# Where the last feed-forward keeps its split weights, where the context gates are applied, and which queue copies the latent keys

## The chip, the cores and the metric

The kernel runs on one core of one Trainium2 chip. The metric is the device time of one execution in microseconds (us); the time before is the median of three runs. One execution was also profiled, and all rows below are from that one. The engines are PE (TensorE: MATMUL, and PEld for its weight loads), DVE (VectorE), ACT (ScalarE), POOL (GpSimd) and SP (SyncE, which issues most of the DMA transfers).

## The reference, cut to what matters

A first block runs on 512 tokens of width 1024: a mixer, a cross attention and a mixture of 16 experts. A second block of two layers follows, on two streams at once: the latent tokens (512, the first block's output) and the context tokens (256). Each layer modulates, projects, attends in three ways (a gated linear attention, a neighborhood attention with 6 heads, "na", and a grouped-query attention with 2 key heads, "ga"), and then does

```python
o = token_mixers(modulate(x, sh1, sc1), ...)   # 1024 wide; the same for the context rows xc
x = layer_norm(ALPHA * x + g1 * (o @ w_out), ln1_g, ln1_b)
a, b = split(modulate(x, sh2, sc2) @ w_ffn_in) # 2 x 2816 wide
x = layer_norm(ALPHA * x + g2 * ((silu(a) * b) @ w_ffn_out), ln2_g, ln2_b)
```

g1 and g2 are rows of 1024 gate factors. The context stream does all of this in layer 0 only; in layer 1 only its keys and values are needed. The latent stream does it in both layers, and the last thing that the program computes is the latent feed-forward of layer 1, here called the last feed-forward.

## The kernel before, in words

**Products.** Every operand is kept as two fp32r parts, high and low, whose sum is the fp32 value, and a product takes three matmuls (`mm3`, L343): high·high, high·low, low·high. A weight chunk (`wchunk`) comes by a 512 KB DMA from SP's queue into a tile `raw`; ACT casts it to `w_h` (L350), and DVE subtracts to get `w_l` (L351, `split`). In the feed-forward's input product (tile `fab`) PE holds the weights `w` still and moves the tokens `hTf` past them; in all token-wise products (tile `pj`) the weights move.

**Where the parts lie.** `raw` and `w` are tiles of a ring pool that lives through the whole program. As the built kernel places them, the latent stages' ring has `raw` from 25 KB on in each partition, `w_h` (3 buffers of 4 KB) at 41 to 53 KB and `w_l` at 53 to 65 KB. A second kind of weight tile, `wk` (16 KB: the hidden activations of the feed-forward, and the weights of a stage's last product in `proj_last`), comes from the pool of the stage, `wk` in the code, and lies between 117 and 167 KB in the latent output projection and feed-forward.

**The last feed-forward.** `ffn` with 4 token tiles takes the 22 hidden blocks in groups of 4, 4, 4, 4, 2, 4. The first three weight chunks go through `in_halves`, which does each product as two halves of 256 columns (it begins when half of the tokens are there): 3 x 24 x 2 = 144 matmuls. The other 41 input chunks are 41 x 24 = 984 matmuls of 512 columns. The output product of the first five groups (18 blocks) is 18 x 4 token tiles x 2 column halves x 3 = 432 matmuls of 512 columns with `w` moving. The last group's output weights are in `wk` (`proj_last`, 96 matmuls). The latent feed-forward of layer 0 is the same program text with other weights.

**The gates.** `wchunk(..., row=g)` lets POOL multiply a raw weight chunk by the gate row in place (L387, `raw<-raw,g2b`) before it is split. All feed-forward output weights, latent and context, go this way, and the context output projection too (`raw<-raw,g1b`). The latent output projection instead multiplies the PSUM result (L2086, `gps<-pj,g1b`) on DVE and adds then (L2088).

**The experts' stage.** From 475 to 1207 us the 16 experts (weights `w`, tiles `h`, `yps`) run in the background of the context stream's layer 0: each foreground weight chunk (`pump`) lets 1.85 steps of the experts follow. POOL gathers the experts' tokens (`hg<-hd,idx`, L1421) in the same queue in which it multiplies. The context products have 2 PSUM buffers and 2 token tiles; DVE takes a finished tile out of PSUM by adding it to x (L2107, `x<-x,pj`).

**The key copies.** `stack_k` writes a pair of heads' keys into halves of the partitions, and `dup_k` (L533) copies each half to the other by DMA, two for `nak_h` and two for `nak_l` of a pair, 128 KB for each issue that the profile lists in the latent stream. They stand in SP's queue, among weight loads (L380), value loads (`navw`, L1657) and others. POOL's queue there holds the rotary multiplies (`gu`, L1763) and the loads of the neighborhood bias (`nab<-in_nabias`, L1621), which wait for a bias buffer that the softmax of two heads earlier has read (`nab` has 2 buffers).

**What sets the order.** The kernel is built with a scheduler that reorders each engine's instructions by a simulated timeline, so a change in one place can move rows in the same stage on all engines.

Of the kernel before, what the change touches and what calls it, by code (L numbers as in the profile page):

```python
# [9 lines left out]
F32 = mybir.dt.float32  # L10
# [5 lines left out]
OP = mybir.AluOpType  # L16
# [4 lines left out]
P = 128  # L21
D = 1024
KT = 8
# [212 lines left out]
def f32(ap):  # L236
    return ap.bitcast(F32)
# [14 lines left out]
class Stream:  # L252


    def __init__(self, tag, ring, raw, hl, mm, sc, scw, mmtag="mm"):
        self.mmtag = mmtag + tag
        self.tag, self.ring, self.raw, self.hl, self.mm, self.sc, self.scw = tag, ring, raw, hl, mm, sc, scw


class Kern:  # L260
# [122 lines left out]
    def wchunk(self, src, kt, n, row=None, w=None):  # L383

        raw = self.wraw(src, kt, n)
        if row is not None:
            self.nc.gpsimd.tensor_tensor(out=raw, in0=raw, in1=row.unsqueeze(1).to_broadcast([P, kt, n]), op=OP.mult)  # L387
        if w is None:
            w = self.hl_tile(self.S.ring, [P, kt, n], "w", bufs=self.S.hl)
        self.split(w, raw)  # L390
        self.pump()
        return w
# [127 lines left out]
        for h in range(2):  # L520
            self.split(HL(vd(dst[0:64, h]), vd(dst[64:128, h])), vs(ps[64 * h:64 * h + 64]), scale)

    def stack_k(self, k, ps):

        for h in range(2):
            r = slice(64 * h, 64 * h + 64)
            self.split(k[r, h], ps[r])
        self.dup_k(k)

    def dup_k(self, k):  # L530
        for t in (k.hi, k.lo):
            for h in range(2):
                self.nc.sync.dma_start(out=f32(t[64 - 64 * h:128 - 64 * h, h]), in_=f32(t[64 * h:64 * h + 64, h]))  # L533

    def scores(self, sc, q, segs):

# [1048 lines left out]
    def na_kq(self, f, l, hT, T, W, lat, full, pool, g, d):  # L1585

        nc = self.nc
        blk = lambda t: t.rearrange("p (b r c) -> p b r c", b=4, c=16)
        k = g["k"] = self.hl_tile(pool, [P, 2, T], "nak", f"nak{f % 2}")
        yield from self.feat_pieces(hT, T, W[:, 384 + f * P:384 + (f + 1) * P], lambda ps: self.stack_k(k, ps[:, :T]))  # L1590
        if not lat:
            d["na_k"].append(self.spill(k, f"nakc{l}{f}"))
        if not full:
            return
        q = g["q"] = pool.tile([P, 2, T], F32R, name="naq", tag=f"naq{f % 2}")

        def ev_q(ps):
            if not lat:
                return self.stack_q(q, ps[:, :T], 0.125)

            for h in range(2):
                t = q[0:64, h], q[64:128, h]
                src = ps[64 * h:64 * h + 64].rearrange("p (r b c) -> p b r c", b=4, c=16)
                nc.scalar.activation(blk(t[0]), src, AF.Copy, scale=-0.125)
                for b in range(4):
                    bs = slice(b * P, (b + 1) * P)
                    nc.vector.scalar_tensor_tensor(out=t[1][:, bs].rearrange("p (r c) -> p r c", c=16), in0=src[:, b],
                                                   scalar=-0.125, in1=f32(t[0][:, bs]).rearrange("p (r c) -> p r c", c=16),
                                                   op0=OP.mult, op1=OP.subtract)
        yield from self.feat_pieces(hT, T, W[:, f * P:(f + 1) * P], ev_q)  # L1610
# [89 lines left out]
    def gqa(self, l, hT, T, W, ctxd, full, d, keep, pool, between, woven):  # L1700
# [3 lines left out]
        nt = T // P  # L1704
# [41 lines left out]
        for i in range(nt):  # L1746
# [38 lines left out]
            for h in range(2):  # L1785
# [1 line left out]
                if full:  # L1787
                    self.split(HL(qS[0:64, :, h, ts], qS[64:128, :, h, ts]), tp[r2, 0:384].rearrange("p (k t) -> p k t", t=P))
                self.split(kS[r2, h, ts], tp[r2, (nb - 1) * P:nb * P])
        self.dup_k(kS)  # L1790
        vs = lambda t, hh, j: t[:, j, 64 * hh:64 * hh + 64]
        if not lat:
            d["ga_k"], d["ga_v"] = self.spill(kS, f"gakc{l}"), self.spill(v, f"gavc{l}")
# [267 lines left out]
    def behind_input(self, hT, pool, works):  # L2061

        t = pool.tile([P, 1], F32, name="bhd", tag="bhd", bufs=1)
        with self.tc.issue_after(self.nc.gpsimd.tensor_copy(t, f32(hT.lo[:, KT - 1, T1 - 1:T1])).ins):
            for f in works:
                f()

    def call(self, f):
        if f is not None:
            f()  # L2070
# [5 lines left out]
    def out_proj(self, l, oT, nt, x, g1b, pool, tile_done):  # L2076

        nc = self.nc
        W = self.A["w_out_2"][l]
        stats = {}  # L2080

        def ev(i, c0, n, ps):
            s = slice(c0, c0 + n)
            if nt == 4:
                t = pool.tile([P, 512], F32, name="gps", tag="gps", bufs=1)
                nc.vector.tensor_tensor(out=t, in0=ps, in1=g1b[:, s], op=OP.mult)  # L2086
                ps = t
            nc.vector.scalar_tensor_tensor(out=x[:, i, s], in0=x[:, i, s], scalar=ALPHA, in1=ps[:, :n], op0=OP.mult, op1=OP.add)  # L2088
            self.ln_stats(stats, x, i, c0)
            if c0 + n == D:  # L2090
                return tile_done(i, stats[i])
        if nt < 4:
            return self.proj_tok(oT, nt, W, lambda *a: self.call(ev(*a)), row=g1b)
        self.proj_tok(oT, nt, W[:, 0:512], ev)
        self.proj_last(oT, nt, W, ev, pool, KT, None, (512,))

    def ffn(self, l, hT, T, x, g2b, pool, tile_done):

        nc, A = self.nc, self.A
        nt = T // P  # L2100
# [3 lines left out]

        def ev(i, c0, n, ps):
            s = slice(c0, c0 + n)
            nc.vector.tensor_tensor(out=x[:, i, s], in0=x[:, i, s], in1=ps[:, :n], op=OP.add)  # L2107

        def ev_last(i, c0, n, ps):
# [5 lines left out]
        for fg in (4, 4, 4, 4, 2, 4):  # L2115
            gT = self.hl_tile(pool, [P, 4, T], "wk", bufs=3 if nt == 4 else 2)
            if f0 == 0 and nt == 4:
                begun = self.in_halves(hT, T, [Wi[:, c:c + P] for c in (0, FF, P)], lambda: self.sc("fab"))
            for f in range(fg):
                ab = []  # L2120
                for z in (0, FF):
                    if begun:
                        ab.append(begun.pop(0))
                        continue
                    c0 = z + (f0 + f) * P
                    w = self.wchunk(Wi[:, c0:c0 + P], KT, P)
                    ab.append(self.sc("fab")[:, 0:T])
                    self.mm3(ab[-1], [(w[:, k, :], hT(k)) for k in range(KT)])
                s = pool.tile([P, T], F32, name="fs", tag="fs", bufs=2)
                nc.scalar.activation(s, ab[0], AF.Silu)  # L2130
                nc.vector.tensor_tensor(out=s, in0=s, in1=ab[1], op=OP.mult)
                self.split(gT[:, f, :], s)
            rows = Wo[f0 * P:(f0 + fg) * P, :]
            f0 += fg
            if f0 < nf or nt < 4:
                self.proj_tok(lambda k: gT[:, k, :], nt, rows, ev if f0 < nf else lambda *a: self.call(ev_last(*a)), kt=fg, row=g2b)
            else:
                self.proj_last(lambda k: gT[:, k, :], nt, rows, ev_last, pool, 4, g2b, (0, 512), lag=2)

# [6 lines left out]
    def layer2(self, l, st, ctxd, full, last=None, keep_hT=False):  # L2146
# [66 lines left out]
        with tpool("xx") as px:  # L2213
# [5 lines left out]
            with tpool("l2") as lp:  # L2219
# [4 lines left out]
                def done1(i, stats):  # L2224
# [5 lines left out]
                        if not lat:  # L2230
                            later.pop()()
                    return rest
                self.out_proj(l, oT, nt, x, gr, wk, done1)
                if lat:
                    self.behind_input(hTf, lp, later)
            oes.close()
            st["hes"].close()
            with tpool("l3") as lp:
                gr = lp.tile([P, D], F32, name="g2b")
                self.ada_bcast(rows, 5, j, gr)  # L2240
                lg, lb = (self.bcast_row(lp, r + 4 * l, n) if j == 0 else None for r, n in ((4, "lng"), (5, "lnb")))
# [20 lines left out]
                    self.affine(x[:, i, :], x[:, i, :], lg, lb)  # L2262
                    nc.sync.dma_start(out=xd[i * P:(i + 1) * P, :], in_=x[:, i, :])
                later = []
                self.ffn(l, lambda k: hTf[:, k, :], T, x, gr, wk, done2)
                if later:
                    self.behind_input(st["hT"], lp, later)
                if last is None:
# [99 lines left out]
```

## Time and profile before

| what | value |
|---|---|
| time, median of 3 runs (lowest, highest) | 2701.52 us (2699.83, 2702.96) |
| the profiled execution's own time, and its span | 2709.36 us, 2707.6 us |
| PE busy, share of the span; mean granted clock | 93%; 0.963 |
| DVE, ACT, POOL busy | 64%, 47%, 15% |
| experts' stage with context layer 0 | 475 to 1207 us |
| context output projection; context feed-forward | 736 to 780 us; 818 to 1207 us |
| latent attention, layer 0; layer 1 | 1390 to 1543 us; 2105 to 2263 us |
| latent feed-forward, layer 0; layer 1 (the last) | 1597 to 1949 us; 2319 to 2671 us |

The bounds of the stages are read from the program's tiles in the order of time. "Busy" counts an engine's instructions; the granted clock is a share of TensorE's full speed. Matmuls overlap in the pipeline: one lasts longer than the distance from its start to the next start, and it is the distance that adds up to the time.

### The profile page before, as it was taken

What the parts mean: (1) busy time and instruction counts of PE and PEld (TensorE: products, weight loads), DVE (VectorE), ACT (ScalarE), POOL (GpSimd) and SP (SyncE); (2) the same over time, 40 slices, a digit from 0 to 9 for tenths busy, and PEclk for the clock granted to TensorE, in tenths of its full rate; (3) what the DMA queues carried; (4) which work ended last, traced back from release to release, by engine and by line L of the source; (5) the groups of instructions that cost most, each with busy time, mean ns of one, the idle gap of its engine ahead of it and who ended that gap; (6) DMA issues with size and microseconds to landing.
All of it is one profiled execution on the core that took longest, in us unless ns stands there. A gap on an engine that the chain in (4) does not pass through costs nothing. (4 is left out here: it accounts for less than half of the span.)

```text
span 2707.6 us, 35926 instructions
## 1 busy us (share of the span) xinstructions
PE 2515.4 (93%) x13176; PEld 1963.8 (73%) x13176; DVE 1725.2 (64%) x3117; ACT 1281.9 (47%) x2389; POOL 418.7 (15%) x304
## 2 busy tenths in 40 slices
PE   8999899798889999988998999999989899999997
PEld 5547575676667888877786588888868666888886
DVE  3346646797687787778786665444567776644446
ACT  4344444576655555556656642222266574422221
POOL 1100000201022121022220023111141200411101
PEclk9999899899999999998999999999989999999999
DMA  7765357588777888767254123333323524233331
GB/s 276 208 203 160 117 192 244 159 268 282 250 241 234 268 276 276 252 222 220 81 156 137 69 87 122 96 94 94 104 86 96 146 82 133 71 101 93 94 93 63
DMA packets 355157, 436.54 MB, mean 161 GB/s; under 512 B 20384, under 2 KB 228128, under 8 KB 354976
## 3 DMA queue, kind: packets, MB, share of 16 engines
q1 hardware_dynamic: 350560, 416.90, 49.1%
q0 software_dynamic: 4416, 17.30, 1.8%
q8 instruction: 105, 1.72, 0.3%
q14 instruction: 76, 0.62, 0.1%
HBM read 387.21 MB, written 38.01 MB: 157 GB/s over the span
## 5 line engine op out<-in xcount | busy, mean ns | idle before, releaser
L351 DVE TENSOR_TENSOR w_l<-raw,w_h 128x1024 fp32r<-128x1024 f32 (+2 forms) x530 | 714.5, 1359 | 465.8 <-ACT w_h L350 456.6
L350 ACT CAST w_h<-raw 128x1024 fp32r<-128x1024 f32 (+2 forms) x530 | 527.5, 1007 | 855.6 <-PE pj L343 272.2
L343 PE MATMUL fab<-hTf_h,w_h 128*128 128x512 f32 (+1 forms) x1104 | 386.2, 351 | 4.1 <-ACT hTf_h L514 3.4
L343 PE MATMUL fab<-hTf_h,w_l 128*128 128x512 f32 (+1 forms) x1104 | 386.7, 351 | 0.5 <-DVE w_l L351 0.4
L343 PE MATMUL fab<-hTf_l,w_h 128*128 128x512 f32 (+1 forms) x1104 | 386.2, 350 | 0.2
L387 POOL TENSOR_TENSOR raw<-raw,g2b 128x1024 f32<-128x1024 f32 x66 | 172.3, 2617 | 708.5 <-DMA raw<-in_w_ffn_out 615.1
L343 PE MATMUL pj<-w_l,hT_h 128*128 128x512 f32 (+3 forms) x608 | 229.8, 379 | 14.1 <-DVE w_l L351 14.1
L343 PE MATMUL pj<-w_h,hT_h 128*128 128x512 f32 (+3 forms) x608 | 222.2, 378 | 14.9 <-ACT w_h L350 9.9
L343 PEld LDWEIGHTS fab<-hTf_h,w_h 128*128 128x128 f32 x1104 | 208.9, 190 | 37.2 <-ACT hTf_h L514 4.5
L343 PEld LDWEIGHTS fab<-hTf_h,w_l 128*128 128x128 f32 x1104 | 209.2, 190 | 32.8 <-DVE w_l L351 1.2
L343 PEld LDWEIGHTS fab<-hTf_l,w_h 128*128 128x128 f32 x1104 | 209.2, 190 | 32.2 <-DVE hTf_l L515 0.6
L343 PE MATMUL pj<-w_h,hT_l 128*128 128x512 f32 (+3 forms) x608 | 225.0, 372 | 0.0
L343 PE MATMUL pj<-w_h,wk_h 128*128 128x512 f32 x376 | 148.5, 401 | 7.9 <-DVE x L2107 4.9
L343 PEld LDWEIGHTS pj<-w_h,hT_h 128*128 128x128 f32 x608 | 118.6, 197 | 45.8 <-ACT w_h L350 13.4
L343 PEld LDWEIGHTS pj<-w_l,hT_h 128*128 128x128 f32 x608 | 120.5, 198 | 42.4 <-DVE w_l L351 18.3
L343 PE MATMUL pj<-w_l,wk_h 128*128 128x512 f32 x376 | 150.0, 400 | 1.1 <-DVE w_l L351 0.9
L343 PE MATMUL pj<-w_h,wk_l 128*128 128x512 f32 x376 | 147.3, 399 | 1.2 <-DVE wk_l L351 1.2
L343 PE MATMUL pf<-hT_h,w_h 128*128 128x512 f32 (+3 forms) x376 | 133.4, 356 | 10.2 <-DVE nak_l L351 3.1
L343 PEld LDWEIGHTS pj<-w_h,hT_l 128*128 128x128 f32 x608 | 120.3, 198 | 22.0 <-issue 5.2
L343 PE MATMUL pf<-hT_h,w_l 128*128 128x512 f32 (+3 forms) x376 | 131.2, 350 | 0.0
L343 PE MATMUL pf<-hT_l,w_h 128*128 128x512 f32 (+3 forms) x376 | 131.2, 350 | 0.0
L577 ACT COPY pT<-ptp 128x512 f32<-128x512 f32 (+3 forms) x184 | 88.5, 497 | 53.5 <-PE ptp L575 52.4
(598 smaller groups left out, 4840.7 us busy)
## 6 DMA issues: line engine op xcount, KB each, us to landing
raw<-in_w SPq DMA_DIRECT2D x192, 512.0 KB
raw<-in_w_ffn_in SPq DMA_DIRECT2D x132, 512.0 KB
raw<-in_w_ada SPq DMA_DIRECT2D x96, 512.0 KB
raw<-in_w_in SPq DMA_DIRECT2D x76, 512.0 KB
raw<-in_w_ffn_out SPq DMA_DIRECT2D x66, 512.0 KB
raw<-in_w_out SPq DMA_DIRECT2D x32, 512.0 KB
yd<-ysb SPq DMA_DIRECT2D x16, 512.0 KB
raw<-in_w_in SPq DMA_DIRECT2D x16, 384.0 KB
```

Source lines behind the costliest of these rows:

```text
L343: self.nc.tensor.matmul(out, lhsT=l, rhs=r, start=first and k == 0 and i == 0, stop=last and k == n - 1 and i == 2, **kw)
L350: nc.scalar.copy(out=hl.hi, in_=src)
L351: nc.vector.tensor_sub(out=hl.lo, in0=src, in1=f32(hl.hi))
L387: self.nc.gpsimd.tensor_tensor(out=raw, in0=raw, in1=row.unsqueeze(1).to_broadcast([P, kt, n]), op=OP.mult)
L577: nc.scalar.copy(out=pT()[:, slice(b0, b0 + bb), ts], in_=tp[:, :bb * P].rearrange("p (b t) -> p b t", t=P))
```

## The change

Three edits are made together.

**Last feed-forward.** The pool for its `wk`, `gT` and `fs` tiles is now the stage's inner pool `l3`, which first allocates room for three pairs of split parts (tag `w`). After the three `in_halves` chunks the stream's `parts` points to that pool, so that every later `w_h`, `w_l` of the last feed-forward goes there: as built, `w_h` at 117 to 129 KB, `w_l` at 129 to 141 KB, the `wk` tiles at 153 to 201 KB; `hTf` (85 to 117 KB) and `raw` stay. Each `w` tile begins, taken modulo 512 bytes, at 224 in place of 352. The out_proj before it takes its `wk` from its own pool, at the same addresses as before.

**Context gates.** The context output projection and feed-forward no longer give `row=` to `wchunk`. A helper `times` multiplies the PSUM result by the gate on DVE into a tile `gps` (one buffer), and the add to x follows from there.

**Key copies.** In the latent stream `dup_k` issues on POOL's queue, not SP's.

```diff
@@ class Stream
+        self.parts = ring
@@ wchunk
-            w = self.hl_tile(self.S.ring, [P, kt, n], "w", bufs=self.S.hl)
+            w = self.hl_tile(self.S.parts, [P, kt, n], "w", bufs=self.S.hl)
@@ dup_k
-    def dup_k(self, k):
+    def dup_k(self, k, eng=None):
         for t in (k.hi, k.lo):
             for h in range(2):
-                self.nc.sync.dma_start(out=f32(t[64 - 64 * h:128 - 64 * h, h]), in_=f32(t[64 * h:64 * h + 64, h]))
+                (eng or self.nc.sync).dma_start(out=f32(t[64 - 64 * h:128 - 64 * h, h]), in_=f32(t[64 * h:64 * h + 64, h]))
@@ na_kq, gqa
+ ... nc.gpsimd if lat else None
@@
+    def times(self, ps, g, pool):
+        t = pool.tile([P, 512], F32, name="gps", tag="gps", bufs=1)
+        self.nc.vector.tensor_tensor(out=t, in0=ps, in1=g, op=OP.mult)
+        return t
@@ out_proj
-            return self.proj_tok(oT, nt, W, lambda *a: self.call(ev(*a)), row=g1b)
+            return self.proj_tok(oT, nt, W, lambda *a: self.call(ev(*a)))
@@ ffn
         def ev(i, c0, n, ps):
             s = slice(c0, c0 + n)
+            if nt < 4:
+                ps = self.times(ps, g2b[:, s], pool)
             nc.vector.tensor_tensor(out=x[:, i, s], in0=x[:, i, s], in1=ps[:, :n], op=OP.add)
...
                 begun = self.in_halves(hT, T, [Wi[:, c:c + P] for c in (0, FF, P)], lambda: self.sc("fab"))
+                if parts is not None:
+                    self.S.parts = parts
...
-                self.proj_tok(lambda k: gT[:, k, :], nt, rows, ev if f0 < nf else lambda *a: self.call(ev_last(*a)), kt=fg, row=g2b)
+                self.proj_tok(lambda k: gT[:, k, :], nt, rows, ev if f0 < nf else lambda *a: self.call(ev_last(*a)), kt=fg,
+                              row=g2b if nt == 4 else None)
@@ layer2
-                self.out_proj(l, oT, nt, x, gr, wk, done1)
+                self.out_proj(l, oT, nt, x, gr, wk if last is None else lp, done1)
...
             with tpool("l3") as lp:
+                if last is not None:
+                    self.hl_tile(lp, [P, KT, P], "w", bufs=3)
...
-                self.ffn(l, lambda k: hTf[:, k, :], T, x, gr, wk, done2)
+                self.ffn(l, lambda k: hTf[:, k, :], T, x, gr, *((wk, done2) if last is None else (lp, done2, lp)))
```

Three places show what moves. On POOL in the experts' stage, before, the gathers of the experts' tokens stand among the gate multiplies of the context weights:

```order
L1421 DMA hg<-hd,idx 128x1024
L387 TENSOR_TENSOR raw<-raw,g2b 128x1024 x4
L1421 DMA hg<-hd,idx 128x1024 x2
L387 TENSOR_TENSOR raw<-raw,g2b 128x1024 x4
L1421 DMA hg<-hd,idx 128x1024
L387 TENSOR_TENSOR raw<-raw,g2b 128x1024 x2
L1421 DMA hg<-hd,idx 128x1024
L387 TENSOR_TENSOR raw<-raw,g2b 128x1024 x2
```

After, POOL has only gathers and the two layer-norm multiplies of the context rows there (lines shift by one and more from here on):

```order
L1422 DMA hg<-hd,idx 128x1024 x6
L2079 TENSOR_TENSOR x<-x,lng 128x1024
L2080 TENSOR_TENSOR x<-x,lnb 128x1024
L1422 DMA hg<-hd,idx 128x1024
L2079 TENSOR_TENSOR x<-x,lng 128x1024
L2080 TENSOR_TENSOR x<-x,lnb 128x1024
L1422 DMA hg<-hd,idx 128x1024 x6
```

All 30 multiplies (8 with `g1b`, 22 with `g2b`) are gone from POOL. On DVE in the context feed-forward, before, a finished pair of tiles is taken out by two adds among the weight splits (`ysb`, `ehT_l` and `es` are the experts'):

```order
L337 COPY ysb<-yps 128x512
L351 TENSOR_TENSOR w_l<-raw,w_h 128x1024
L351 TENSOR_TENSOR ehT_l<-etp,ehT_h 128x512
L351 TENSOR_TENSOR w_l<-raw,w_h 128x1024
L2107 TENSOR_TENSOR x<-x,pj 128x512 x2
L351 TENSOR_TENSOR ehT_l<-etp,ehT_h 128x512
```

After, the same place has two multiplies and two adds, and splits stand between them:

```order
L352 TENSOR_TENSOR w_l<-raw,w_h 128x1024
L352 TENSOR_TENSOR ehT_l<-etp,ehT_h 128x512
L352 TENSOR_TENSOR w_l<-raw,w_h 128x1024
L2071 TENSOR_TENSOR gps<-pj,g2b 128x512
L352 TENSOR_TENSOR ehT_l<-etp,ehT_h 128x512
L2113 TENSOR_TENSOR x<-x,gps 128x512
L352 TENSOR_TENSOR w_l<-raw,w_h 128x1024
L2071 TENSOR_TENSOR gps<-pj,g2b 128x512
```

DVE has 28 multiplies more in this stage (4 in the output projection, 24 in the feed-forward). On POOL in a latent layer's attention, before, the rotary multiplies are followed by the bias loads of heads 2 to 5 alone:

```order
L1763 TENSOR_TENSOR gu<-gsq,tsq 128x12x16 x2
L1763 TENSOR_TENSOR gu<-gsq,tsk 128x4x16 x2
L1763 TENSOR_TENSOR gu<-gsq,tsq 128x12x16 x2
L1763 TENSOR_TENSOR gu<-gsq,tsk 128x4x16 x2
L1621 DMA nab_13153<-in_nabias 128x768
L1621 DMA nab_13869<-in_nabias 128x768
```

After, sixteen key copies of that layer stand among them, first between the rotary multiplies and then between bias loads:

```order
L1764 TENSOR_TENSOR gu<-gsq,tsq 128x12x16 x2
L1764 TENSOR_TENSOR gu<-gsq,tsk 128x4x16 x2
L534 DMA gak_h<-gak_h 64x512
L534 DMA gak_l<-gak_l 64x512
L1622 DMA nab_13179<-in_nabias 128x768
L534 DMA gak_h<-gak_h 64x512
L534 DMA gak_l<-gak_l 64x512
L534 DMA nak_h<-nak_h 64x512
L534 DMA nak_l<-nak_l 64x512
L534 DMA nak_h<-nak_h 64x512
L534 DMA nak_l<-nak_l 64x512
L1622 DMA nab_13895<-in_nabias 128x768
```

SP's queue has 16 rows less in each latent layer. In the last feed-forward PE's order does not change, and only a few splits move by a place on ACT and DVE; what changes is the addresses.

## Rows read from the trace of the kernel before

**Rows 1.** The page: busy time of each engine.
```profile
PE 2515.4 (93%) x13176; PEld 1963.8 (73%) x13176; DVE 1725.2 (64%) x3117; ACT 1281.9 (47%) x2389; POOL 418.7 (15%) x304
```

**Rows 2.** Stretches: length, busy us of PE, PEld, DVE, ACT, POOL, clock, DMA share, GB/s.
```profile
818.00:1207.00 389.00, 366.36 (x2087) 314.86 (x2086) 301.23 (x322) 215.98 (x274) 70.22 (x32) 0.97 0.78 253
...
2105.00:2263.00 158.00, 137.35 (x774) 98.35 (x773) 114.81 (x333) 106.56 (x267) 11.75 (x17) 0.95 0.39 113
...
2319.00:2671.00 352.00, 350.38 (x1574) 286.04 (x1573) 170.50 (x161) 97.84 (x127) 80.08 (x31) 1.00 0.31 93
```

**Rows 3.** PE groups by line and shape, 2332 to 2671: xcount | busy us, mean ns.
```profile
L343 PE MATMUL fab<-hTf_h,w_h 128*128 128x512 f32 x328 | 129.6, 395 | 0.0
...
L343 PE MATMUL pj<-w_h,wk_h 128*128 128x512 f32 x144 | 56.9, 395 | 0.0
...
L343 PE MATMUL fab<-hTf_h,w_h 128*128 128x256 f32 x21 | 6.6, 316 | 0.0
```

**Rows 4.** PE by time (start us, us), ring weights: first and last of 87 starts.
```profile
2399.78 0.40 PE L343 MATMUL fab<-hTf_h,w_h 128*128 128x512 f32 x1
...
2419.84 0.40 PE L343 MATMUL fab<-hTf_h,w_l 128*128 128x512 f32 x1
```

**Rows 5.** PE by time, "wk" weights: first and last of 40 starts.
```profile
1573.16 0.39 PE L343 MATMUL pj<-wk_h,hT_l 128*128 128x512 f32 x1
...
1582.00 0.39 PE L343 MATMUL pj<-wk_h,hT_l 128*128 128x512 f32 x1
```

**Rows 6.** One stretch of rows 5, columns of rows 2.
```profile
1574.00:1577.00 3.00, 3.00 (x14) 2.47 (x14) 2.90 (x6) 0.00 (x0) 0.00 (x0) 1.00 0.54 158
```

**Rows 7.** POOL group, 736 to 1207: busy us, mean ns | idle before, releasers.
```profile
L387 POOL TENSOR_TENSOR raw<-raw,g2b 128x1024 f32<-128x1024 f32 x22 | 58.5, 2664 | 215.7 <-DMA raw<-in_w_ffn_out 156.1 <-DVE w_l L351 37.1 <-DVE wk_l L351 19.7
```

**Rows 8.** DVE group, same stretch and columns.
```profile
L351 DVE TENSOR_TENSOR w_l<-raw,w_h 128x1024 fp32r<-128x1024 f32 (+1 forms) x205 | 276.2, 1370 | 92.7 <-ACT w_h L350 89.2 <-PE fab L343 2.7
```

**Rows 9.** Tile w_l, same stretch: duration ns min/median/max.
```profile
L351 DVE TENSOR_TENSOR w_l<-raw,w_h x205: 422/1221/3439, 734.8 to 1201.8; 128x1024 fp32r<-128x1024 f32 x101, 128x256 fp32r<-128x256 f32 x1, 128x512 fp32r<-128x512 f32 x1
```

**Rows 10.** POOL, DVE and PE by time before one PE gap [idle before <-releaser].
```profile
931.22 2.67 POOL L387 TENSOR_TENSOR raw<-raw,g2b 128x1024 f32<-128x1024 f32 x1 [5.54 <-DMA raw<-in_w_ffn_out]
...
931.55 2.62 DVE L351 TENSOR_TENSOR wk_l<-fs,wk_h 128x256 fp32r<-128x256 f32 x1
...
934.69 2.35 DVE L351 TENSOR_TENSOR w_l<-raw,w_h 128x1024 fp32r<-128x1024 f32 x2
936.96 1.27 DVE L2107 TENSOR_TENSOR x<-x,pj 128x512 f32<-128x512 f32 x2
...
937.78 0.47 PE L343 MATMUL pj<-w_h,wk_h 128*128 128x512 f32 x1 [2.30 <-DVE x L2107]
```

**Rows 11.** PE by time: three other gaps of this kind.
```profile
1009.51 0.50 PE L343 MATMUL h<-w_l,ehT_h 128*128 128x512 f32 x1 [2.08 <-DVE w_l L351]
...
1077.12 0.80 PE L343 MATMUL pj<-w_h,wk_h 128*128 128x512 f32 x1 [2.17 <-DVE x L2107]
...
1186.29 0.73 PE L343 MATMUL pj<-w_h,wk_h 128*128 128x512 f32 x2 [2.70 <-ACT w_h L350]
```

**Rows 12.** Tile gps: the gate multiply out of PSUM, ns min/median/max.
```profile
L2086 DVE TENSOR_TENSOR gps<-pj,g1b x16: 672/679/693, 1568.2 to 2318.9; 128x512 f32<-128x512 f32 x16
```

**Rows 13.** SP and DVE by time in the attention of latent layer 1.
```profile
2134.82 4.32 SPq L533 DMA_DIRECT2D gak_h<-gak_h  x1
...
2155.09 0.47 SPq L533 DMA_DIRECT2D nak_l<-nak_l  x1
...
2145.27 0.69 DVE L351 TENSOR_TENSOR nak_l<-pf,nak_h 64x512 fp32r<-64x512 f32 x1 [0.44 <-ACT nak_h L350]
```

**Rows 14.** POOL by time there.
```profile
2148.97 0.54 POOL L1621 DMA_DIRECT2D nab<-in_nabias  x1 [12.76 <-DVE rr L566]
2165.57 0.54 POOL L1621 DMA_DIRECT2D nab<-in_nabias  x1 [16.06 <-DVE nmx L654]
```

**Rows 15.** PE waits, 2105 to 2263: us in total, times, longest.
```profile
PE sc L543 <- DMA nak_l<-nak_l: 1.9, 1, 1.9
```

More of the change, by code (lines that the diff above doesn't have):

```diff
@@ L521, in stack_q, with stack_k @@
             self.split(HL(vd(dst[0:64, h]), vd(dst[64:128, h])), vs(ps[64 * h:64 * h + 64]), scale)
-    def stack_k(self, k, ps):
+    def stack_k(self, k, ps, eng=None):
         for h in range(2):
@@ L527, in stack_k @@
             self.split(k[r, h], ps[r])
-        self.dup_k(k)
-    def dup_k(self, k):
+        self.dup_k(k, eng)
+    def dup_k(self, k, eng=None):
         for t in (k.hi, k.lo):
             for h in range(2):
-                self.nc.sync.dma_start(out=f32(t[64 - 64 * h:128 - 64 * h, h]), in_=f32(t[64 * h:64 * h + 64, h]))
+                (eng or self.nc.sync).dma_start(out=f32(t[64 - 64 * h:128 - 64 * h, h]), in_=f32(t[64 * h:64 * h + 64, h]))
     def scores(self, sc, q, segs):
@@ L1589, in na_kq @@
         k = g["k"] = self.hl_tile(pool, [P, 2, T], "nak", f"nak{f % 2}")
-        yield from self.feat_pieces(hT, T, W[:, 384 + f * P:384 + (f + 1) * P], lambda ps: self.stack_k(k, ps[:, :T]))
+        yield from self.feat_pieces(hT, T, W[:, 384 + f * P:384 + (f + 1) * P], lambda ps: self.stack_k(k, ps[:, :T], nc.gpsimd if lat else None))
         if not lat:
@@ L1789, in gqa @@
                 self.split(kS[r2, h, ts], tp[r2, (nb - 1) * P:nb * P])
-        self.dup_k(kS)
+        self.dup_k(kS, nc.gpsimd if lat else None)
         vs = lambda t, hh, j: t[:, j, 64 * hh:64 * hh + 64]
@@ L2083, in ev @@
             s = slice(c0, c0 + n)
[L2084 to L2088, printed above, removed]
+            nc.vector.scalar_tensor_tensor(out=x[:, i, s], in0=x[:, i, s], scalar=ALPHA, in1=self.times(ps, g1b[:, s], pool),
+                                           op0=OP.mult, op1=OP.add)
             self.ln_stats(stats, x, i, c0)
@@ L2092, in out_proj, with ffn @@
         if nt < 4:
-            return self.proj_tok(oT, nt, W, lambda *a: self.call(ev(*a)), row=g1b)
+            return self.proj_tok(oT, nt, W, lambda *a: self.call(ev(*a)))
         self.proj_tok(oT, nt, W[:, 0:512], ev)
         self.proj_last(oT, nt, W, ev, pool, KT, None, (512,))
-    def ffn(self, l, hT, T, x, g2b, pool, tile_done):
+    def ffn(self, l, hT, T, x, g2b, pool, tile_done, parts=None):
         nc, A = self.nc, self.A
```

## The prediction

> **What bounds the kernel now.** The page comes first: PE is busy for 93% of the span, the next engine for 64% [rows 1]. So a microsecond is saved where PE's own instructions get shorter or where PE stands still, and the table by stretches says which holds where [rows 2]. In the last feed-forward PE is busy for 350.4 of 352 us at full clock, DVE for less than half of it, and the DMA engines for under a third. Nothing but the matmuls themselves sets that stage's time. In the context feed-forward, beside the experts, PE lacks 389 − 366.4 = 22.6 us, with DVE at 301 us and the DMA at 0.78. In the attention of latent layer 1 it lacks 20.7 of 158 us, and neither DVE (114.8) nor ACT (106.6) is full there: a chain of waits, not an engine.
>
> **First part: the addresses of the last feed-forward's weights.** How far apart do its matmuls start? From the first to the last of 87 consecutive ones, 2419.84 − 2399.78 = 20.06 us over 86 steps, 233.3 ns each [rows 4]. The same shape with `wk` weights, which lie above 117 KB, starts every (1582.00 − 1573.16)/39 = 226.7 ns [rows 5]. In both, PE is never idle and the clock is full. Could the difference be traffic rather than place? In 3 us of the closer starts DVE was busy for 2.90 us and the DMA engines at 0.54 [rows 6], more than in the wider ones, so the load on the memory does not order them. What differs is where the operands are: where starts are 233 ns apart, one operand is in the ring (41 to 65 KB); where they are 227 apart, both are above 69 KB. Whether the region or the offset within 512 bytes does it, the rows do not say; the change moves both to the values of the latter rows.
>
> The Trainium skill speaks against this part: its page "SBUF — State Buffer", section "Who interferes with whom", says that PE never waits on anyone for SBUF, and names no place that is slower. By that rule the two distances would be equal and this part worth nothing; by the rows they are 233.3 and 226.7 ns, and the rows decide.
>
> How many matmuls gain? 984 of `fab` and 432 of `pj` with 512 columns are moved; the mean durations of both kinds are alike at 395 ns, 328 and 144 times for one of the three products each, as counted in the code [rows 3]. The 144 half-width ones and the last group keep their places. Gain per matmul: 233.3 − 226.7 = 6.6 by these two stretches. The 40 close starts had hardly a cast beside them, and a part of the stage's matmuls may run at other distances, so I take 6.0: 1416 × 6.0 ns = **8.5 us**. Bounds: 0 if place does nothing, 1416 × 6.6 = 9.3 above. Will something else now be late? DVE has 180 us free in the stage and the DMA 0.69, so the 2.4% faster PE stays covered. The added wait of the new tiles, that the pool above the token tiles be free, is met before: PE works through the `in_halves` chunks, still in the ring.
>
> **Second part: the context gates.** Removed from POOL in the context feed-forward: 22 multiplies of 2664 ns, 58.5 us [rows 7]; 8 more fall in the output projection before. POOL is no bound, but two things hang on these multiplies. One is the chain: a gated chunk waits for POOL before ACT may cast it, and ACT takes chunks in order. The other is DVE: a 128x256 subtraction that began 0.33 us after a multiply took 2.62 us and ended 0.28 us after it [rows 10], where the splits of 128x1024 have a median of 1221 ns and a longest of 3439 [rows 9]. So DVE stands still while POOL multiplies. Over the stage the mean is 1370 ns against that median [rows 8, 9]: 205 × 0.149 = 30.5 us of DVE lost in `w_l` alone.
>
> The Trainium skill's rule for it (the page "SBUF — State Buffer", section "Who interferes with whom") is that a DVE instruction with two SBUF inputs contends with a GpSimd one that reads SBUF, by an exclusive lock. The trace agrees: 2.62 us beside a multiply of 2.67 us.
>
> Added to DVE: 28 multiplies out of PSUM of 0.68 us [rows 12], 19.0 us. DVE therefore gives back 30.5 − 19.0 = 11.5 us in the stage. What is that worth on PE? I count only gaps of PE that I can follow to a POOL multiply. In the first, POOL's multiply holds the subtraction until 934.17, the two splits behind it end at 937.0, the adds that free PSUM come after them, and PE waited 2.30 us [rows 10]. Three more, of 2.08, 2.17 and 2.70 us, end on a delayed `w_l`, an `x` add and a cast of a gated chunk [rows 11]. Together 9.25 us. Against it: for each pair of tiles the second PSUM tile is now freed one DVE operation (0.68 us) later when an add is placed before it; 14 pairs × 0.68 = 9.5 us if PE waited for every one. PE has the experts' matmuls to do between them, and the gaps on `x` adds before came only where DVE had been held, so I charge a third, 3.2 us. Sum: 9.25 − 3.2 = **6 us** gained. Bounds: a gain of 22.6 us (all that PE lacks), a loss of 9.5 us (no gap goes, every pair waits). I take a value near the middle because the reordering touches the whole stage and the DMA at 0.78 can take some of it back.
>
> **Third part: the key copies.** SP loses 32 issues of about 0.47 us, POOL gets them at the 0.54 us of its bias loads [rows 14]. On SP a copy can be stuck: one `gak_h` took 4.32 us to issue, and a `nak_l` that DVE had finished at 2145.27 + 0.69 = 2145.96 (the last split of that pair) left at 2155.09, 9 us late [rows 13]. PE waited for a copy of `nak_l` for 1.9 us, once, in this layer [rows 15], and I count on nothing in layer 0. On POOL nothing blocks these copies longer than the bias loads do, and the pair finished at 2145.96 is through, at four issues, by 2148.1, before the bias load at 2148.97 was free to go [rows 14]. So the 1.9 us go, some 0.4 us come back where a rotary multiply stands behind a copy: **1.5 us** gained. Bounds: a gain of 4.3 us (the stuck issue was on the way too), a loss of one bias wait in a layer, 16.06 us [rows 14].
>
> **The sum.** 8.5 + 6 + 1.5 = 16 us off the profiled execution's 2709.4 (span 2707.6), so 2693.4. The median of the three runs is 7.8 us lower, 2701.5; less 16 it is 2685.5, and I say **2686 us**.
>
> **The rivals.** A measurement of this kernel tells 0.2%, 5.4 us, from no change.
>
> *Place does nothing.* For: the 40 close starts are of another stage, and a short sample. Against: two stages' worth of durations, 395 ns without exception where `w` is an operand [rows 3]. The first part falls to 0: 2701.5 − 7.5 = 2694. The Trainium skill's sentence above gives this time. Chance 0.12.
>
> *The experts' stage fills up with other waits.* With 0.78 of the DMA busy and a new order of all rows, the gaps that POOL caused come back behind weight loads. For: DVE's 92.7 us of idle time there wait for casts, which wait for data too [rows 8]. The second part falls to 0: 2701.5 − 10 = 2691.5. Chance 0.19.
>
> *The gate multiply costs PE its PSUM tiles.* For: context products have two tiles only. No gap goes, each pair waits: 2701.5 − 8.5 − 1.5 + 9.5 = 2701, no change. Chance 0.08.
>
> *Key copies stuck behind a bias load: slower.* POOL takes its queue in order. A copy behind a bias load that waits up to 16.06 us for the softmax [rows 14] reaches PE that much later, and the scores of the next pair of heads wait. For: the new order has copies of the third pair behind such a load. Against: in the order of before these loads were released about when the copies' sources were written. It turns the sum when the two layers lose 14.5 + 5.4 = 20 us; at 12.76 us each they lose 25.5, and the time is 2701.5 − 14.5 + 25.5 = 2712.5. Chance 0.05.
>
> **How the numbers follow.** The forecast's own case has the remaining 0.56, at 2678 to 2692. The other cases end at 2691.5, 2694, 2701 and 2712.5. Leaving out the last (0.05), most of the one before (0.07) and what may lie below the forecast's case (0.06), the range is **2676 to 2700**. Faster by over 0.2% means below 2696.1: 0.53 of the forecast's 0.56, 0.10 of the first rival's 0.12 and 0.17 of the second's 0.19 make 0.80. Slower means above 2706.9: the last rival and 0.01 for the PSUM one, 0.06. The rest, 0.14, is within.
>
> **What would show it.** Of part one: durations of `fab` and `pj` matmuls of the last feed-forward below 395 ns, starts 227 ns apart, the stage 8 to 9 us shorter, while the feed-forward of latent layer 0, which is untouched, stays as it is. Of part two: `w_l` splits without a long tail between 818 and 1207, a mean near 1.22 us, 28 `gps` multiplies, and fewer microseconds between the start and the end of the experts' stage. Of part three: no PE wait for a `nak` copy, and the two latent attentions within 3 us of before. The prediction is wrong if the starts in the last feed-forward remain 233 ns apart, if PE waits for `x` or `gps` tiles after each context pair, or if bias loads land late and the softmax waits.

## The result, and the profile after

The changed kernel took 2657.8 us (median of 4 runs, 2650.7 to 2668.2) against 2700.7 us before in the same session: ratio 0.985 (95% interval 0.982 to 0.988), some 42 us shorter. The forecast was 16 us, so the direction was right and the size was not; the time lies below the range.

The first view to take is the table by stages. It is made of start times of PE's matmuls in the two traces: each row is the time from one named start to the next.

| from, to (first or last PE start of a tile) | before, us | after, us | difference |
|---|---|---|---|
| program start to the first expert product `h` | 541.4 | 532.0 | −9.4 |
| to the first context `fab` | 277.4 | 272.9 | −4.5 |
| to the last expert product `yps` (context feed-forward) | 380.2 | 349.3 | −30.9 |
| to the first latent `glG`, layer 0 | 130.5 | 134.8 | +4.3 |
| to the first `sc<-nak`, layer 0 | 77.1 | 77.2 | 0 |
| attention and out_proj, layer 0, to the first `fab` | 190.8 | 188.9 | −1.9 |
| first to last `fab`, layer 0 (unchanged code) | 351.1 | 352.7 | +1.6 |
| to the first `sc<-nak`, layer 1 | 175.3 | 174.1 | −1.2 |
| attention and out_proj, layer 1, to the first `fab` | 194.9 | 189.0 | −5.9 |
| first to last `fab`, layer 1 (the last feed-forward) | 352.4 | 342.2 | −10.2 |
| to the end | 36.5 | 35.9 | −0.6 |

The two profiled executions differ by 58.7 us, more than the medians do. One cause is seen in the first row: at 331 us, in the cross attention, which the change doesn't touch, the two are already 4.6 us apart, and in the twelve kernels run below the first `h` starts anywhere from 531.5 to 541.1 us, with no relation to the edit. So those 9.4 us are mostly the spread of executions. The third row is where the forecast was far off, but it does not hold the same work in both kernels: after the change 29 of the experts' `h` products start ahead of the first `fab`, and eight transposes after the last `yps`. From the first `h` to the first latent `glG` (the second to the fourth row) the same 3867 matmuls start in both. These are the two stretches of equal work, before and then after, in the columns of [rows 2] (length; busy us of PE, PEld, DVE, ACT, POOL with instruction counts; granted clock; DMA share; GB/s):

```profile
541.40:1329.50 788.10, 712.08 (x3872) 591.70 (x3871) 611.49 (x846) 471.10 (x709) 140.77 (x79) 0.95 0.75 245
...
532.00:1288.90 756.90, 707.33 (x3868) 594.05 (x3867) 592.50 (x878) 474.09 (x718) 63.42 (x51) 0.95 0.78 256
```

PE stands idle for 76.0 us in the first and 49.6 us in the second. Here are the three stretches that answer to [rows 2], after:

```profile
804.00:1154.00 350.00, 345.08 (x2041) 302.19 (x2040) 272.67 (x320) 205.09 (x256) 6.13 (x6) 1.00 0.83 270
2063.00:2215.00 152.00, 133.57 (x772) 96.42 (x771) 114.78 (x333) 106.19 (x266) 20.84 (x33) 0.96 0.41 118
...
2271.00:2613.00 342.00, 340.24 (x1576) 284.28 (x1575) 171.34 (x161) 97.65 (x127) 81.37 (x31) 1.00 0.32 96
```

The first of them ends with the last `yps`; the one in [rows 2] goes on for 8 us, in which PE is busy for less than half. Before, the stretch from the first `fab` to the last `yps` was:

```profile
818.80:1199.00 380.20, 362.90 (x2074) 312.66 (x2074) 293.59 (x308) 209.82 (x261) 67.86 (x29) 0.98 0.79 254
```

So in the context feed-forward PE lacks 4.9 us where it lacked 17.3, DVE is busy for 272.7 us where it was for 293.6, although it has the gate multiplies more, and the granted clock is 1.00, not 0.98. In the last feed-forward nothing but the length has changed: PE is as full as before.

The groups of PE that answer to [rows 3], 2284 to 2613 us (xcount | busy us, mean ns):

```profile
L344 PE MATMUL fab<-hTf_h,w_h 128*128 128x512 f32 x328 | 127.6, 389 | 0.0
L344 PE MATMUL pj<-w_h,wk_h 128*128 128x512 f32 x144 | 56.0, 389 | 0.0
...
L344 PE MATMUL fab<-hTf_h,w_h 128*128 128x256 f32 x21 | 5.9, 281 | 0.0
```

Each full-width matmul is 6 ns shorter. The splits that answer to [rows 8, 9], from the first `fab` to the last `yps`, 804.8 to 1154.1 us (first the group, then the tile's minimum, median and maximum in ns):

```profile
L352 DVE TENSOR_TENSOR w_l<-raw,w_h 128x1024 fp32r<-128x1024 f32 x167 | 200.0, 1216 | 67.3 <-ACT w_h L351 66.8
```

```profile
L352 DVE TENSOR_TENSOR w_l<-raw,w_h x167: 372/1219/1227, 804.9 to 1152.7; 128x1024 fp32r<-128x1024 f32 x166, 128x256 fp32r<-128x256 f32 x1
```

The tail of 3439 ns is gone there: the longest split is 1227 ns, 8 ns above the median. Of the wider stretch of [rows 8, 9] only three splits above 1.4 us remain (2452 to 3084 ns, at 787 to 799 us), each beside one of POOL's layer-norm multiplies.

### The profile page after: what moved, and what is told of

Its sections match the earlier page's. It is cut to its first block, busy times and chain, and to the rows that moved or that the text cites. A ratio compares the mean times of both kernels' runs of the same rounds, so it can differ in the third digit from the quotient of the medians.

```text
span 2648.9 us, 35931 instructions
## 1 busy us (share of the span) xinstructions
PE 2488.8 (94%) x13176; PEld 1958.0 (74%) x13176; DVE 1707.1 (64%) x3145; ACT 1282.5 (48%) x2389; POOL 358.4 (14%) x306
## 4 chain that ended last, share of the span: by engine, by line
PE 58%; DVE 7%; ACT 3%; DMA 3%; issue 2%; POOL 1%; DVEq 0%; ACTq 0%; POOLq 0%
PE fab L344 22%; PE pj L344 20%; PE h L344 3%; PE oat L636 3%; PE yps L344 2%; PE pf L344 2%; DVE w_l L352 2%; PE ptp L576 2%; PE sc L543 1%; ACT w_h L351 1%; DMA raw<-in_w 1%; PE glG L1982 1%; PE sc L544 1%; PE tp L501 1%; DMA nab<-in_nabias 1%
## 5 line engine op out<-in xcount | busy, mean ns | idle before, releaser
L352 DVE TENSOR_TENSOR w_l<-raw,w_h 128x1024 fp32r<-128x1024 f32 (+2 forms) x530 | 686.9, 1304 | 445.0 <-ACT w_h L351 432.9
L388 POOL TENSOR_TENSOR raw<-raw,g2b 128x1024 f32<-128x1024 f32 x44 | 115.0, 2623 | 484.3 <-DMA raw<-in_w_ffn_out 461.4
```

Source lines behind the costliest of these rows:

```text
L352: nc.vector.tensor_sub(out=hl.lo, in0=src, in1=f32(hl.hi))
```

## The experiments

The ratios are to the kernel before, run in the same session; one per mille is 2.7 us.

**One part at a time.** Each of the three is the kernel before with one part of the change's diff (`parts` and `l3`; `times` without `row=`; `nc.gpsimd if lat else None`).

> The first part alone (split weights of the last feed-forward in the middle of SBUF). Theory A, place counts and only there: the last feed-forward takes 342 us in place of 352 (fab and pj durations 389 ns, not 395), nothing else moves, and the time falls by 8 to 10 us, to about 2691. Rival, that a new order or a freed pool helps elsewhere too: more than 15 us. Rival, that the gain in the profile of the full change is chance: within 3 us of before.

Measured: ratio 0.997 (0.996 to 0.998), 7.8 us shorter; the last feed-forward 343.3 us, the durations 389 ns, the other stages as before within their spread. Theory A holds.

> The second part alone (context gates applied to PSUM on DVE). Theory A, POOL's gate multiplies cost the experts' stage far more than the 6 us forecast, by DVE held, by late casts and by the clock that falls after PE gaps: context feed-forward 318 to 325 us in place of 351, total 25 to 40 us shorter, about 2665 to 2675. Rival, the part is worth the 6 us of the forecast and the rest of the gain is the third part or chance: about 2695.

Measured: 0.990 (0.988 to 0.991), 28 us shorter. The stretch that the expectation means, first to last context `fab`, takes 321.4 us (350.7 before); first context `fab` to last `yps`, the table's row, takes 350.8 (380.2 before). This part alone is worth more than four times its term, as theory A has it; which of A's three causes takes how much, this run does not say.

> The third part alone (latent key copies on POOL's queue). Forecast: 1.5 us shorter, both attentions within 3 us of before, 2699. Theory B, the queue of SP held the second latent attention: 5 to 6 us shorter there (from 195 to 189 us), total 2694. Rival, copies behind bias loads: longer by 5 us or more.

Measured: 0.999 (0.997 to 1.000), 3.0 us shorter with an interval that includes no change. The stage shows it better. Over all traces, attention and out_proj of layer 1 took 193.6 to 194.9 us in the three kernels with the copies on SP and 186.7 to 191.5 us (mean 189.5) in the eleven with them on POOL; in layer 0 the means are 190.4 and 190.5. So it is worth some 5 us in layer 1 and nothing in layer 0. Theory B was nearly right about the stage (190.4 us in this kernel); the whole time can't tell it from the forecast. Together the three single parts give 39 us; the whole change gave 42.

**What the address does.** The last feed-forward's split weights stay in the middle, 128 bytes higher:

```diff
                 if last is not None:
+                    lp.tile([P, 32], F32, name="pad0")
                     self.hl_tile(lp, [P, KT, P], "w", bufs=3)
+                    lp.tile([P, 96], F32, name="pad1")
```

> The full change, with 128 bytes of padding ahead of the three pairs of split parts in the last feed-forward, so that they lie in the middle of SBUF but begin at 352 modulo 512 bytes, as in the ring; wk tiles at 224 modulo 512 as in the full change. Theory region: fab and pj durations stay at 389 ns and the stage at 342 us. Rival, the offset within 512 bytes: 395 ns and 352 us, 9 us longer than the full change.

Measured: 352.7 us for the stage, total 0.988 (0.985 to 0.990), 8 us longer than the full change. The group of its last feed-forward, 2350 to 2620 us:

```profile
L344 PE MATMUL fab<-hTf_h,w_h 128*128 128x512 f32 x274 | 108.1, 395 | 0.0
```

The place in SBUF is not the cause; where a tile begins within 512 bytes is. Two kernels then move the ring and the other left tiles by a few bytes. In the first, w in the ring begins at 224 and hTf and the last feed-forward's w at 256:

```diff
+        self.cst.tile([P, 8], F32, name="pad0")
         self.ring = ctx.enter_context(tc.tile_pool(name="ring", bufs=2))
...
+        self.cst2 = ctx.enter_context(tc.tile_pool(name="cst2", bufs=1))
-        self.lvl = self.cst.tile([P, 5, 32], U8, name="lvl")
+        self.lvl = self.cst2.tile([P, 5, 32], U8, name="lvl")
```

> The full change with the ring shifted down by 128 bytes, so that w in the ring begins at 224 modulo 512 bytes (by moving one small constant tile behind the ring); the tiles after the ring shift up by 32 bytes, to 256 modulo 512 (hTf, wk, the last feed-forward's w). Theory offset (352 is costly, 224 is not, the region is of no account): fab in the feed-forward of latent layer 0 falls from 395 to 389 ns and the stage from 352 to 342 us, and every other stage with ring weights gains 6 ns a matmul, some 15 us more over mixer, experts and projections. Rival region: layer 0 stays at 395 ns and 352 us. Of 256 for the other tiles no theory says anything.

Measured: 0.983 (0.981 to 0.985). The two feed-forwards, layer 0 (1650 to 1890 us) and then the last (2345 to 2615 us):

```profile
L346 PE MATMUL fab<-hTf_h,w_h 128*128 128x512 f32 x232 | 91.6, 395 | 0.0
...
L346 PE MATMUL fab<-hTf_h,w_h 128*128 128x512 f32 x286 | 111.3, 389 | 0.0
```

This is the miss that settled it. The held w at 224 was cheap in the full change beside hTf at 224, and is dear here beside hTf at 256; and 256 beside 256 is cheap. It is not the offset of an operand that counts but the distance between the two.

The second has 160 bytes of padding ahead of the ring (`self.cst.tile([P, 40], ...)`) and 128 after it, so that all these tiles begin at 0:

> The full change with padding so that ring and all left tiles after it (w, hTf, wk, w of the last feed-forward) begin at 0 modulo 512 bytes; 288 bytes more in use. Theory offset in its simplest form, that an operand is dear when its rows cross a line: 0 is at least as good as 224, and both latent feed-forwards have 389 ns or less. Rival, that only some property of 224 makes it cheap: 395 ns in both latent feed-forwards, 10 us longer than the full change.

Measured: 0.980 (0.978 to 0.983); 343.4 us in layer 0 and 344.6 us in layer 1, with all operands at 0 (layer 0, 1650 to 1890 us):

```profile
L347 PE MATMUL fab<-hTf_h,w_h 128*128 128x512 f32 x242 | 94.1, 389 | 0.0
```

From these a rule was formed, that the two operands must begin at the same place modulo 256 bytes, and tested in two kernels that differ in the first part. Both have w in the ring at 224 and the left tiles after it at 480 (as e5_ring224, with a `pad1` of 224 bytes after the ring):

> The full change, with the ring at 224 modulo 512 bytes and the left tiles after it at 480 (one small tile moved behind the ring, 32 and 224 bytes of padding), so that moving and held operand begin at the same place modulo 256 bytes in all feed-forwards, projections and mixers; only the experts' products, and the context's input projection, stay apart. Theory relative offset (a matmul starts every 227 ns when its two operands begin at the same place modulo 256 bytes, else every 233): both latent feed-forwards take 342 us, projections and mixers gain 5 to 6 ns a matmul, total 15 to 20 us shorter than the full change, about 2640. Rival, an absolute offset of 0 or 224 modulo 512 is needed: layer 0 stays at 352 us, since hTf is at 480.

> As e9_align, but without the first part: the last feed-forward's split weights stay in the ring. Theory relative offset: the same time as e9_align within 2 us, the last feed-forward at 342 to 344 us with its weights in the ring. Rival, the move out of the ring has a worth of its own: 352 us there and 8 to 10 us longer than e9_align.

Measured: 0.980 (0.978 to 0.983) and 0.981 (0.978 to 0.983), medians 2649.1 and 2645.3 us. Layer 0's `fab` range takes 343.4 us in both; the last feed-forward takes 344.5 us with its weights moved and 343.4 us with them in the ring. The group there in the kernel that doesn't move them (2340 to 2600 us):

```profile
L346 PE MATMUL fab<-hTf_h,w_h 128*128 128x512 f32 x271 | 105.4, 389 | 0.0
```

So the move out of the ring is worth nothing by itself once the operands are aligned, and layer 0 gets the same 9 us. The sum missed its expectation: 12 us below the full change, not 15 to 20. The stages between the feed-forwards did not get shorter by more than their spread although their matmuls are aligned too. e8_left0 says the same: there the latent streams' `pf` and `pj<-w,hT` still start every 233 ns, in e9_align every 227 to 228, and the two kernels take the same time. That the stages between wait for other engines was seen before in [rows 2]; that this is why was not tested. These two, and e8_left0, are the shortest kernels of the study; their intervals (0.978 to 0.983) overlap a little with the change's (0.982 to 0.988).

**What the gate multiplies cost.** All four kernels here are the full change with work added to the 30 context chunks that POOL multiplied before; nobody reads what is added. First, POOL multiplies again, but nothing waits for it:

```diff
             w = self.hl_tile(self.S.parts, [P, kt, n], "w", bufs=self.S.hl)
+        if shadow is not None:
+            p, row = shadow
+            t = p.tile([P, kt, n], F32, name="shw", tag="shw", bufs=1)
+            self.nc.gpsimd.tensor_tensor(out=t, in0=raw, in1=row.unsqueeze(1).to_broadcast([P, kt, n]), op=OP.mult)
```

> The full change, and POOL multiplies each of the 30 gated context chunks all the same, into a scratch tile that nobody reads (POOL reads raw as before; the cast does not wait for it, but raw is free only when POOL has read it). Theory port, that the loss was DVE held by POOL's reads: the context feed-forward goes back from 320 to 340 us or more, w_l again with a tail to 3 us, total 20 to 30 us longer than the full change. Theory chain, that the loss was the cast waiting for the multiply: within 5 us of the full change.

Measured: 0.999 (0.997 to 1.000), 38 us longer than the full change: the whole gain of the part is gone, and more. First `fab` to last `yps` 376.1 us, first to last `fab` 340.7 (319.9 in the full change). Its POOL group and its splits there (817 to 1193 us):

```profile
L394 POOL TENSOR_TENSOR shw<-raw,g2b 128x1024 f32<-128x1024 f32 x22 | 62.6, 2844 | 194.0 <-DMA raw<-in_w_ffn_out 192.3 <-issue 1.5
```

```profile
L352 DVE TENSOR_TENSOR w_l<-raw,w_h x169: 425/1218/3434, 818.0 to 1191.7; 128x1024 fp32r<-128x1024 f32 x168, 128x256 fp32r<-128x256 f32 x1
```

The tail to 3.4 us is back. This kernel also keeps raw until POOL has read it. The next one doesn't: POOL multiplies the gate rows with themselves (`in0=row` in place of `in0=raw`).

> As e6_port, but POOL multiplies the gate rows with themselves into the scratch tile, so that it reads no raw and holds no weight buffer; it may run the multiplies in other places than e6_port. Theory port: 30 multiplies of 2.5 us hold DVE all the same, 20 to 40 us longer than the full change, w_l with a tail above 2 us. Rival, that e6_port lost by raw buffers that POOL kept: within 6 us of the full change.

Measured: 0.994 (0.992 to 0.996), 25 us longer than the full change, 371 us from first `fab` to last `yps`, the longest split 2911 ns. POOL's 22 multiplies with `g2b` ran in a bunch (823 to 888 us) and most of the loss is back all the same. Whether the 13 us less than in e6_port come from `raw`, which is free sooner, or from the other places of the multiplies, is not separated. The next was to be the opposite case, where a cast waits for POOL but POOL reads nothing:

```diff
+        if shadow is not None:
+            for _ in range(2):
+                self.nc.gpsimd.memset(f32(w.hi), 0.0)
```

> The full change, and POOL fills w_h of each of the 30 context chunks with zeros, twice, before ACT casts into it (a cast waits for POOL, POOL writes but reads nothing from SBUF; it waits for the w buffer, so somewhat more than the multiply did). Theory chain: the context feed-forward goes back to 340 us or more. Theory port: within 6 us of the full change, w_l without a tail.

Measured: 0.986 (0.984 to 0.988), 3.5 us longer than the full change, within the intervals of both; 347.2 us from first `fab` to last `yps`, 332.0 from first to last `fab`, and no tail, though 20 of the splits ran beside a memset (814 to 1162 us):

```profile
L352 DVE TENSOR_TENSOR w_l<-raw,w_h x169: 416/1224/1228, 813.2 to 1160.2; 128x1024 fp32r<-128x1024 f32 x168, 128x256 fp32r<-128x256 f32 x1
```

So POOL's writes don't hold DVE. On the chain it says little. A memset waits for the `w` buffer, not for the chunk's data, so it can be done before the data is there. This is how long ACT stood idle for POOL, before (818.8 to 1199 us) and then in this kernel (814.6 to 1161.8 us; us in total, times, longest):

```profile
ACT w_h L350 <- POOL raw L387: 44.3, 17, 6.2
```

```profile
ACT w_h L351 <- POOL w_h L393: 4.6, 4, 1.5
```

A tenth of the old waiting was put back, so what the chain cost before stays untested. The last one asks what DVE's time is worth in a stage where DVE is busy for less than 80%: no multiply of gates on POOL, and the same multiply on DVE (`self.nc.vector.tensor_tensor`):

> The full change, and DVE (not POOL) multiplies each of the 30 gated context chunks into a scratch tile that nobody reads: about 30 x 1.2 = 36 us more work on DVE, about what POOL's reads took from it before, with POOL idle. Theory DVE-bound loop (weight loads wait for DVE's split to free raw, so that DVE's time is the stage's time though it is busy for under 80%): 20 to 35 us longer than the full change. Theory that only a hold at the wrong moment costs, as in the four PE gaps of the forecast: within 10 us of the full change.

Measured: 0.995 (0.993 to 0.997), 29 us longer than the full change; 372.8 us from first `fab` to last `yps`. DVE's added work, 700 to 1200 us:

```profile
L394 DVE TENSOR_TENSOR shw<-raw,g2b 128x1024 f32<-128x1024 f32 x22 | 26.9, 1224 | 24.7 <-DMA raw<-in_w_ffn_out 24.7
...
L394 DVE TENSOR_TENSOR shw<-raw,g1b 128x1024 f32<-128x1024 f32 x8 | 9.8, 1219 | 1.9 <-DMA raw<-in_w_out 1.9
```

36.7 us of plain work on DVE cost 29 us. DVE also stood 24.7 us ahead of these multiplies until their `raw` landed, as the first line shows; but its idle time in the stage as a whole did not grow (73.8 of 372.8 us, 77.3 of 349.3 in the full change).

## Why the prediction was right in direction and wrong in size

**First part: right.** The term of 8.5 us came out at 7.8 by time and 8 to 10 in the stage, at the durations that were named as the sign. The reason stayed open in the prediction, region or offset, and is now known to be neither: it is the distance between the two operands' beginnings modulo 256 bytes. The `fab` cases together (hTf, w, modulo 512; mean ns): 224, 352: 395, in either place; 224, 224: 389; 256, 224: 395; 256, 256: 389; 0, 0: 389; 480, 224: 389; 480, 480: 389. That the moved weights came to lie at hTf's own offset was luck in part: the same move is worth nothing in e4_mid352. The prediction weighed the sentence of the Trainium skill ("SBUF — State Buffer", section "Who interferes with whom") that PE never waits on anyone. No run here shows another engine holding PE, so the sentence stands; but the time of a matmul does depend on where its operands lie, by 6 ns in 395, which one reading of it had excluded.

**Second part: the step that failed is "What is that worth on PE? I count only gaps of PE that I can follow to a POOL multiply".** The term was 6 us and measured 28. That DVE stands still while POOL multiplies was named rightly: e6_port and e11_port2 bring the hold back, without a cast that waits for POOL, and the loss with it. What was wrong is the price of DVE's time. The four gaps came to 9.25 us; over the equal work PE's idle time fell by 26.4 us in the two executions compared, and by 18 us on average (74 to 76 us in the three kernels without this part, 50 to 59 in the seven with it and no work added). A view of before that the prediction does not use is the waits of SP's queue. Here they are for the kernel before, 818 to 1199 us, and then for the one after, 804 to 1154 us (us in total, times, longest):

```profile
SPq L380 <- DVE w_l L351: 237.4, 141, 8.2
```

```profile
SPq L381 <- DVE w_l L352: 194.8, 138, 4.9
```

Most weight loads wait for a split on DVE to free their buffer. That is a way for a held split to delay a load, for the load to delay a later cast, and for that to delay a later matmul, long after the multiply. The view alone does not show that it binds: the changed kernel has 138 such waits too, and PE lacks only 4.9 us. The price is shown by e13_dve: 29 us for 36.7 us of DVE work, 0.8 us for 1. The prediction had DVE give back 11.5 us (of the 30.5 us that it counted as lost in `w_l`, 4.5 stand beside POOL's layer-norm multiplies, which stay); over the equal work its busy time fell by 19.0 (611.5 to 592.5), among it 22 `wk_l` at 685 ns that now take 417 (5.9 us, left out). At that rate this is 15 us of time.

The other 13 us are not accounted for by DVE's time. Over the equal work e6_port, e11_port2 and e13_dve have 46, 38 and 30 us more of DVE's busy time than the full change and take 36, 24 and 27 us more; the kernel before has only 19 us more and takes 31 us more. What fits is the other thing that the prediction named and did not price, the chain: casts stood 44.3 us for POOL. No run here puts that back, so its share stays open. The rows also did not cover four of the multiplies, ahead of 736 us.

One cost beside the gaps was put at nothing, the clock. Next to three of the four gaps the granted clock was 0.50 (1.2 GHz) for 13.6 us together (columns of [rows 2]):

```profile
939.20:942.60 3.40, 3.40 (x9) 2.67 (x9) 1.23 (x1) 1.05 (x1) 0.22 (x1) 0.50 0.53 154
1010.90:1014.30 3.40, 3.40 (x10) 2.62 (x9) 3.40 (x4) 1.40 (x2) 0.00 (x0) 0.50 0.74 239
1075.70:1082.50 6.80, 5.38 (x13) 4.23 (x14) 4.30 (x6) 1.96 (x3) 1.62 (x1) 0.50 0.96 342
```

PE was busy for 12.2 of these 13.6 us, so some 6 us went there, by an estimate from these lines. The changed kernel has no such stretch in its context feed-forward. Over the equal work the gain is less clear: the length times what the granted clock lacks of 1 is 39.3 us before and 41.0 after, and 37 to 43 us in the three kernels without this part against 29 to 41 in the seven with it (means 40 and 34).

The charge of 3.2 us for PSUM tiles freed late was too high: PE waited 0.2 us on `gps` in the whole context feed-forward after. And the bound of 22.6 us, "all that PE lacks", was no bound: it took one stretch, 818 to 1207 us, and the 8 multiplies with `g1b` stand ahead of it, at 636 to 770 us.

**Third part: right in sign, small in size.** 1.5 us forecast, about 5 us in layer 1's attention by all traces, 3.0 us by time with an interval that includes zero. The wait on a `nak` copy in [rows 15] is gone: among PE's waits of the changed kernel in 2063 to 2215 us no DMA of a key copy appears, while the three kernels with the copies on SP have 1.8 to 2.4 us of it. The rest of the 5 us stays open. It is not simply the stuck `gak_h` issue of [rows 13], which the bound had added: in those three kernels it takes 4.1 to 4.6 us in both layers, and layer 0 gained nothing. The sign "the two latent attentions within 3 us of before" failed for layer 1. No copy was stuck long behind a bias load: with copies behind them, the bias loads waited 2.1 us at most.

**The rivals.** "Place does nothing" is refuted in its form here (e1_last_ffn), and true in another (e12_align_nomove). "The stage fills up with other waits", "the gate multiply costs PE its PSUM tiles" and "key copies stuck behind a bias load" did not occur. No rival was on the side where the result fell: each of them made the gain smaller.

## What to carry to other kernels

Before valuing an engine's freed time by the gaps it leaves on the bounding engine, look at who waits for it in the DMA queue, and, where that is most of the loads, add plain work to it in a test: here an engine at 77%, whose instructions free the load buffers, was worth 0.8 us for 1. A POOL operation that reads SBUF takes the time of DVE's two-input operations beside it, so its price is at least DVE's, not POOL's. Compare stages over equal work, for a scheduler moves work across their bounds. Where PE is full, compare the start-to-start distance of like matmuls, and set moving and held operand at the same offset modulo 256 bytes: padding of a few bytes does what a move to another pool did.

## What the runs showed of the hardware that was not expected

A 512-column fp32r matmul starts every 227 ns if its two operands begin at the same offset modulo 256 bytes, and every 232 to 233 ns at the `fab` distances tried otherwise (32 and 128 bytes), up to 2.8% of PE's time; the durations are 389 and 395 ns. The region of SBUF made no difference (e4_mid352, e12_align_nomove); traffic was not varied by itself. POOL's memsets did not hold DVE's two-input subtractions (longest 1227 ns of the 20 that ran beside one in e7_chain), its multiplies did (longest 3434 ns in e6_port); the Trainium skill ("SBUF — State Buffer", section "Who interferes with whom") says that such a DVE instruction contends with a GpSimd one that reads SBUF and not with one that only writes, and the traces agree.
